# Transposing split queries and keys by float32r products with a unit matrix, in a kernel of two blocks on one core

## The chip, the core and the metric

The kernel runs on one core of a Trainium2 chip. Its metric is device time in microseconds, the median of several runs. Five engines work side by side, each through its own instructions in order: TensorE (PE; its loads of the stationary operand are listed as PEld), VectorE (DVE), ScalarE (ACT), GpSimd (POOL) and SyncE (SP), which here issues the loads from memory. TensorE writes to PSUM only, and other engines carry its results from there.

## What is computed

The reference runs two blocks of two layers each on 256 tokens of 1024 channels, with 256 tokens of context beside them. The change lies in the second block, in the mixers of its two layers. Both are attention over 64-wide heads whose queries and keys are normed by head and, for the latent tokens, rotated. The first layer ("even") has grouped heads, half of them with a window; the second ("odd") takes the difference of two attentions per head.

```python
def _odd_mixer(hx, hc, w_in, w_out, qn, kn, lq1, lk1, lq2, lk2, subln_w, lam_init, cos, sin, with_ctx):
    ...
    def heads(p, use_rope):
        b, n = p.shape[:2]
        q, k, v = jnp.split(p, [qs, 2 * qs], axis=-1)
        q = _rms(q.reshape(b, n, HEADS_C, 2, d), qn)
        k = _rms(k.reshape(b, n, HEADS_C, 2, d), kn)
        if use_rope:
            q, k = _rope(q, cos, sin), _rope(k, cos, sin)
        return q, k, v.reshape(b, n, HEADS_C, 2 * d)

    q_x, k_x, v_x = heads(hx @ w_in, True)
    q_c, k_c, v_c = heads(hc @ w_in, False)
    ...
    o_x = _diff_attend(q_x, jnp.concatenate([k_c, k_x], axis=1), jnp.concatenate([v_c, v_x], axis=1), lam)
```

All of it is float32. The kernel carries the large products in float32r, a float32 with fewer mantissa bits, and so splits each operand in two parts, hi (the rounded value) and lo (what is left), and adds three products.

## The kernel before

Activations lie with channels on partitions for the projections: aH and aL are hi and lo of the normed input. Weights come in by SyncE as 512 KB tiles wraw; ScalarE rounds them to whi (L392) and VectorE subtracts to get wlo (L397). mm3 (L411 to L413) issues the three products of hi and lo.

The attention needs queries and keys with the head's 64 channels on partitions, but their projection (tile pin, made by chunk) gives tokens on partitions. So qk (L1069) takes a chunk's result for two tiles of 128 tokens and four heads: a norm by head on VectorE, gains and rotation, the last product with the norm's factor at L1090, and then the split. For queries ScalarE rounds into q_st (L1093), and VectorE subtracts into its other half (L1094). For keys there is one tile k_st for each tile of tokens; ScalarE writes the hi part twice (L1106) and VectorE the lo part twice (L1107). Both tiles are float32r already, and share one pair of buffers.

The transposes come later (the function late that qk returns): stream runs them in the midst of the next chunk, after its third step. For each tile of tokens of queries there is one call of turned, and for keys two, one for hi (into ks0) and one for lo (into ks1). turned (L1123) issues four transposes of 128x128, one per head, into one PSUM bank (ptq), and ScalarE copies the bank into qs or ks (L1128):

```python
        pt = self.turn_tile(pp, "ptq")
        for h, a in enumerate(srcs):
            nc.tensor.transpose(out=pt[:, h, :], in_=a.bitcast(F32).rearrange("p e d -> p (e d)"), identity=self.ident)
        nc.scalar.copy(out=dst, in_=pt)
```

turn_tile (L1116) gives two banks by turns; the same two banks serve the transposes of the probabilities (ptp) and of the results (pto). scores (L1130) multiplies a query tile with ks0 and ks1 (L1134, L1135).

In the even layer the first k chunk, the v chunk and so on go pair of tiles by pair of tiles, and the later q chunks are woven into the attention of the group before. In the odd layer there are four pairs of heads j; while j's attention runs, the k and q chunks of j + 1 are woven in. So a pair has two sets of key transposes, 16 each (context, then latent tokens), and one of 8 for the queries.

The order on each engine is not the program's own order. A scheduler runs through the instructions by priority with durations that it assumes, and takes for each engine what is ready by then. The order is then fixed: on the chip each engine goes through it and waits wherever something is not ready.

Of the kernel before, what the change touches and what calls it, by code (L numbers as in the profile page):

```python
# [10 lines left out]
F32 = mybir.dt.float32  # L11
# [7 lines left out]
D = 1024  # L19
# [11 lines left out]
# columns of the per-partition vectors of a layer of the first block  # L31
# [7 lines left out]
# rows that are the same for each token, first block  # L39
RV = {"bv": (0, 512), "bs": (512, 256), "slg": (768, 256), "slb": (1024, 256)}  # L40
NRV = 1280
# the same, second block
# [3 lines left out]
# constants  # L46
CS = {"ident": (0, 128), "mf": (128, 128), "mb": (256, 128)}
NCS = 384
# constants of the first block's gates: selectors of a head's row, resets of the running sums
CG = {"sel": (0, 512), "reset": (512, 512)}  # L50
NCG = 1024
# norm gains
# [3 lines left out]
# form A tiles (128 columns) and form B chunks (256 columns) of the first block's input projection, in order  # L56
IN1 = ["gates", "k0", "k1", "k2", "k3", "q0", "q1", "q2", "q3", "V0", "V1", "a0", "g0", "a1", "g1", "u0", "u1", "S0",
       "o0", "o1", "o2", "o3"]
# how far an item of the first block's mixer falls behind in the order of priority
LOW, LOWC = 300, 600  # L60
# parts of the first layer's modulation that the tensor engine computes; the pairs of its shift tiles that it does as well
PE_C = [0, 1, 4]
SHPE = (1,)
# priority of the split of weights, by phase
WPRI = {"m1": 50, "ev": 400}
# other work per step of a phase, and the products woven into the attention's stages
PACE = {"m1": 0.0, "w1": 5.5, "o": 0.0, "f00": 5.0, "d00": 3.0, "f01": 1.0, "d01": 1.0, "f10": 3.0, "d10": 3.0}
RATE = {"ev": 0.7, "evo": 1.5, "od": 1.8, "odo": 1.0, "odv": 5.0}
# order of the work in the first block's mixer, by layer
# [18 lines left out]
class Net:  # L88
# [36 lines left out]
    # ---- modulation vectors: n on partitions, one dot product along the free axis each  # L125
# [6 lines left out]
    def cvec_pe(self, s, row):  # L132
        """The same for the first block, spread by the tensor engine."""
        nc = self.nc
        t = self.cv[s] = self.mp.tile([128, D], F32, tag="cv", name=f"cv0{s}")
        for h in range(2):
            p = self.mm_tile("pcv")
            nc.tensor.matmul(out=p, lhsT=self.ones[0:1, :], rhs=row[0:1, 512 * h:512 * h + 512], start=True, stop=True)
            nc.scalar.activation(out=t[:, 512 * h:512 * h + 512], in_=p, func=AF.Silu)
# [10 lines left out]
    def mod_gain(self, b, l, c, s):  # L150
        """A norm's gain times one plus the scale."""
# [4 lines left out]
    def mod_tile(self, b, l, j, streams, w=None):  # L156
        """Tile j of the 48 of a layer."""
# [14 lines left out]
    def mod_pe(self, c, q, room, pr, pm):  # L172
        """Tiles 2 q and 2 q + 1 of the first layer's part c on the tensor engine, for both streams: rows, then turned."""
# [12 lines left out]
    def mod_take(self, c, j0, j1, pm):  # L186
        """Tiles j0 to j1 of the part c, with the bias and with the norm's gain."""
# [10 lines left out]
    def start(self):  # L198
        """The first norm, tile by tile as its scales (on the tensor engine) and shifts become known."""
# [63 lines left out]
    def work(self, n):  # L263
        """Some of the modulation vectors that later layers need: as many dot products as credit allows."""
# [10 lines left out]
    def need(self, key):  # L275
        """The vectors of the key, and all before them in the queue."""
        while any(x[2] == key for x in self.bg):
            self.credit = self.bg[0][0]
            self.work(0.0)
# [4 lines left out]
    # ---- norms  # L284
    def rsq(self, x, n, scale, alone=False, x2=None, lim=None):
        """1 / sqrt(x * scale + eps) for [128, n]: a first guess from the exponent's bits, then two steps.
        With x2, then also 1 / sqrt(x2 + eps * (x * scale + eps)). With lim, 1 / sqrt(min(x, lim) + eps / scale)."""
# [18 lines left out]
        # the last step to the third order: y * (3/8 h^2 - 5/4 h + 15/8) with h = a * y^2  # L306
# [7 lines left out]
    def rstd_rows(self, sqs, n, scale, pc, pb, sqs2=None):  # L314
        """1 / sqrt(scale * (sum over partitions and tiles of sqs) + eps) for n tokens, on all partitions of pb.
        With sqs2, a second norm of the first one's result as well: the product of both factors, from the sums of the
        first one's squares and of those times its gains (and 1 / D)."""
# [15 lines left out]
    def squares(self, src, cols, scales=(None,)):  # L333
        """For each of the scales (by channel) two tiles whose sum over partitions is that of the squares over all channels."""
# [19 lines left out]
    def norm(self, src, cols, A, B, room=None):  # L354
        """aH + aL = src * rstd * A + B."""
# [25 lines left out]
    # ---- weights: loaded, split in two parts that one pass of the tensor engine carries exactly  # L381
# [18 lines left out]
    def more_weights(self, pool, n):  # L400
        """Further room for n weight tiles, from a pool of the phase."""
# [6 lines left out]
    def mm3(self, out, wh, wl, xh, xl, start, stop):  # L408
        """W.T @ x: weights stationary."""
# [5 lines left out]
    def accA(self, outs, ws, xs, cols, first=True, last=True):  # L415
        """For each output its weights; the pieces of the weights are [128, 128] each, for the tiles in xs."""
# [8 lines left out]
    def accB(self, out, ws, t):  # L425
        """x.T @ W: 128 tokens stationary; two pieces of weights, [128, 4, 256] each."""
# [11 lines left out]
    def order(n, colsets, head, tail):  # L438
        """Chunks by ranges of tokens; the first `head` and the last `tail` go range by range."""
# [7 lines left out]
    # ---- residual update by a projection: x += g * (W.T y)  # L447
# [11 lines left out]
    def part(self, p, w, ks, cols, first, last):  # L459
        """The tiles ks of a product over aH + aL, for the range of tokens cols."""  # L460
# [6 lines left out]
    def out_early(self, src, cols, ks):  # L467
        """The first tiles of a projection, as far as the tiles ks of its input reach."""
# [14 lines left out]
    def unscaled(self, pool, key):  # L483
        """The norm's input times its gains, without the factor by token, in two parts; the shifts as one more token.
        The first products take this, so that they need not wait for the factors."""
# [22 lines left out]
    def scaled(self, pool, p, rb, name):  # L508
        """A product with the unscaled input: times the factors by token, and the shifts' part."""
# [79 lines left out]
    # ---- the first block's mixer  # L589
    def mixer1(self, l, pace):  # L590
        nc, tc = self.nc, self.tc
        last = l == 1
        with ExitStack() as ctx:
# [43 lines left out]
            # rows 0..3: forward heads, 32..35: backward heads; the second half of the partitions likewise  # L637
# [10 lines left out]
            def interior(j):  # L648
                """Where the convolution's input goes: (context, latents) without the padding."""
# [61 lines left out]
            # -- the gates' running sums and maxima  # L711
            with tc.tile_pool(name="gp", bufs=1) as gp:
# [41 lines left out]
                # minus these, so that the selectors' minus makes it up  # L754
# [13 lines left out]
            # -- mLSTM chunks  # L768
# [10 lines left out]
            def step(c, d_, first, update, output):  # L779
# [4 lines left out]
                # minus M of each head, on all partitions  # L784
# [62 lines left out]
            def hnorm(c):  # L847
                """The sum of both directions, rms norm by head."""
# [8 lines left out]
            def gated(c):  # L857
                """The normed sum, times the output gate (into the gate's tiles)."""
# [106 lines left out]
    # ---- the second block  # L965
    def rows2(self, mx):
        rows = mx.tile([128, NR2], F32, name="rows")
        self.nc.sync.dma_start(out=rows, in_=self.i["rv2"].to_broadcast([128, NR2]))
        self.rot = mx.tile([128, 256], F32, name="rot")
# [3 lines left out]
    def tables(self, mx, rows, names, tag, scale=1.0):  # L973
        """Rotation tables with gains, [128, 2, 4, 64], for the head gains `names` (one, or one for each of four heads)
        times a power of two."""
# [19 lines left out]
    # ---- streams of instructions that are woven into each other; each yields what it has cost on the tensor engine  # L995
    def ahead(self, srcs):
        """Weights in order, each asked for one before its use."""
# [7 lines left out]
    def chunk(self, ws, toks, done):  # L1005
        """256 columns of an input projection for pairs of tiles of tokens; done gets each pair's result."""
# [15 lines left out]
    def fill_late(self, n):  # L1022
        """What waits for the vector engine's part of a chunk."""
# [5 lines left out]
    def stream(self, *parts):  # L1029
        """Chunks one after the other; what a chunk leaves to the tensor engine comes in the midst of the next one."""  # L1030
# [10 lines left out]
    def weave(self, main, fill, rate):  # L1041
        """rate: the fill's cost for one of main's."""
# [14 lines left out]
    def pipe(units):  # L1057
        """Software pipeline over units of four stages: (stage, cost) each."""
# [576 lines left out]
```

## Time and profile before

| | |
|---|---|
| median of 3 runs | 2061.7 us (2060.18 to 2063.29) |
| span of the profiled execution | 2055.1 us (the time around it is not listed apart) |
| instructions | 34137 |
| TensorE / VectorE / ScalarE busy | 2010.6 / 1545.2 / 924.5 us |
| mean granted TensorE clock | 0.994 |
| float32 transposes of L1127 | 256 records, from 1074.3 to 1818.1 us |

The span runs from the first to the last instruction of one profiled execution. Busy time of TensorE counts overlapping records once, and ends of its products are modelled, so its pace is read from the starts of successive rows. In a timeline, neighbouring instructions of one line are merged into a row with a count. An idle time stands in brackets behind a row, with what ended it.

### The profile page before, as it was taken

What the parts mean: (1) busy time and instruction counts of PE and PEld (TensorE: products, weight loads), DVE (VectorE), ACT (ScalarE), POOL (GpSimd) and SP (SyncE); (2) the same over time, 40 slices, a digit from 0 to 9 for tenths busy, and PEclk for the clock granted to TensorE, in tenths of its full rate; (3) what the DMA queues carried; (4) which work ended last, traced back from release to release, by engine and by line L of the source; (5) the groups of instructions that cost most, each with busy time, mean ns of one, the idle gap of its engine ahead of it and who ended that gap; (6) DMA issues with size and microseconds to landing.
All of it is one profiled execution on the core that took longest, in us unless ns stands there. A gap on an engine that the chain in (4) does not pass through costs nothing.

```text
span 2055.1 us, 34137 instructions
## 1 busy us (share of the span) xinstructions
PE 2010.6 (98%) x13196; PEld 1784.5 (87%) x13196; DVE 1545.2 (75%) x3105; ACT 924.5 (45%) x1612; POOL 85.7 (4%) x103
## 2 busy tenths in 40 slices
PE   8999999999999899999999999999999999999999
PEld 3798779888888799999998789888888889999999
DVE  6997789987898768987877667777653487788554
ACT  4324544222322346744556675322222266666443
POOL 0000010000001000200100002000000200001000
PEclk9999999999999999999999999999999999999999
DMA  7532265678766332576651015446752231216554
GB/s 295 181 103 92 97 232 176 211 248 295 235 216 198 111 102 94 170 263 212 202 171 61 22 41 186 154 149 223 260 170 71 70 112 64 73 54 224 182 157 134
DMA packets 98182, 324.22 MB, mean 158 GB/s; under 512 B 11418, under 2 KB 14234, under 8 KB 98020
## 3 DMA queue, kind: packets, MB, share of 16 engines
q1 hardware_dynamic: 98020, 322.04, 47.7%
q8 instruction: 104, 1.70, 0.3%
q14 instruction: 58, 0.48, 0.1%
HBM read 320.95 MB, written 1.05 MB: 157 GB/s over the span
## 4 chain that ended last, share of the span: by engine, by line
PE 89%; DVE 6%; ACT 2%; DMA 1%; issue 1%; SPq 0%; POOL 0%; ACTq 0%; POOLq 0%; DVEq 0%
PE pg L411 6%; PE pd L411 6%; PE pd L413 6%; PE pd L412 6%; PE pu L413 6%; PE pg L412 6%; PE pu L412 6%; PE pg L413 6%; PE pu L411 6%; PE pin L411 5%; PE pin L413 5%; PE pin L412 5%; PE pov L1223 2%; PE ptq L1127 2%; DVE wlo L397 1%; PE po L411 1%
## 5 line engine op out<-in xcount | busy, mean ns | idle before, releaser
L392 ACT CAST whi<-wraw 128x1024 fp32r<-128x1024 f32 (+2 forms) x443 | 429.5, 973 | 797.0 <-PE pu L412 188.9
L397 DVE TENSOR_TENSOR wlo<-wraw,whi 128x1024 fp32r<-128x1024 f32 (+2 forms) x443 | 502.5, 1138 | 155.0 <-ACT whi L392 152.3
L165 DVE CUSTOM_DVE_ANT_0 junk<-mw,cv,modb 128x1024 bf16<-128x1024 f32 x272 | 349.6, 1285 | 51.3 <-DMA mw<-in_modw 45.2
L411 PE MATMUL pd<-hH,whi 128*128 128x256 f32 (+1 forms) x748 | 245.4, 328 | 0.0
L412 PE MATMUL pd<-hL,whi 128*128 128x256 f32 (+1 forms) x748 | 245.1, 328 | 0.0
L413 PE MATMUL pd<-hH,wlo 128*128 128x256 f32 (+1 forms) x748 | 244.8, 327 | 0.0
L411 PE MATMUL pg<-aH,whi 128*128 128x256 f32 (+1 forms) x704 | 233.8, 332 | 0.3 <-ACT aH L374 0.3
L413 PE MATMUL pu<-aH,wlo 128*128 128x256 f32 (+1 forms) x704 | 233.5, 332 | 0.3 <-DVE wlo L397 0.3
L412 PE MATMUL pg<-aL,whi 128*128 128x256 f32 (+1 forms) x704 | 233.6, 332 | 0.0
L412 PE MATMUL pu<-aL,whi 128*128 128x256 f32 (+1 forms) x704 | 233.2, 331 | 0.0
L411 PE MATMUL pu<-aH,whi 128*128 128x256 f32 (+1 forms) x704 | 233.2, 331 | 0.0
L413 PE MATMUL pg<-aH,wlo 128*128 128x256 f32 (+1 forms) x704 | 233.2, 331 | 0.0
L412 PEld LDWEIGHTS pd<-hL,whi 128*128 128x128 f32 x748 | 142.2, 190 | 12.2
L411 PEld LDWEIGHTS pd<-hH,whi 128*128 128x128 f32 x748 | 142.4, 190 | 12.0
L413 PEld LDWEIGHTS pd<-hH,wlo 128*128 128x128 f32 x748 | 142.2, 190 | 12.0
L411 PE MATMUL pin<-whi,aH 128*128 128x256 f32 x512 | 150.0, 293 | 1.4 <-ACT aH L374 1.1
L412 PE MATMUL pin<-wlo,aH 128*128 128x256 f32 x512 | 148.0, 289 | 0.0
L413 PE MATMUL pin<-whi,aL 128*128 128x256 f32 x512 | 147.2, 289 | 0.3 <-DVE aL L375 0.2
L411 PEld LDWEIGHTS pg<-aH,whi 128*128 128x128 f32 x704 | 133.7, 190 | 13.2 <-ACT aH L374 0.5
L413 PEld LDWEIGHTS pu<-aH,wlo 128*128 128x128 f32 x704 | 133.7, 190 | 13.1 <-DVE wlo L397 0.5
L413 PEld LDWEIGHTS pg<-aH,wlo 128*128 128x128 f32 x704 | 133.8, 190 | 12.6
L412 PEld LDWEIGHTS pg<-aL,whi 128*128 128x128 f32 x704 | 133.8, 190 | 12.5
(339 smaller groups left out, 4150.8 us busy)
## 6 DMA issues: line engine op xcount, KB each, us to landing
wraw<-in_wgu SPq DMA_DIRECT2D x176, 512.0 KB, 4.4
mw<-in_modw SPq DMA_DIRECT2D x168, 512.0 KB, 4.2
wraw<-in_win SPq DMA_DIRECT2D x92, 512.0 KB, 3.5
wraw<-in_wdn SPq DMA_DIRECT2D x64, 384.0 KB, 3.5
wraw<-in_wout SPq DMA_DIRECT2D x47, 512.0 KB, 3.5
wraw<-in_wdn SPq DMA_DIRECT2D x64, 320.0 KB, 3.4
mn<-in_modn SPq DMA_DIRECT2D x18, 512.0 KB, 5.6
mn<-in_modw SPq DMA_DIRECT2D x6, 512.0 KB, 7.3
```

Source lines behind the costliest of these rows:

```text
L165: r = nc.vector.tensor_tensor_reduce(out=junk, in0=w, in1=self.cv[s], scale=1.0, scalar=self.mb_t[:, 2 * b + l, j:j + 1], op0=ALU.mult, op ...
L392: nc.scalar.copy(out=hi[:, :n], in_=raw[:, :n])
L397: nc.vector.tensor_tensor(out=lo[:, :n], in0=raw[:, :n], in1=hi[:, :n], op=ALU.subtract)
L411: mm(out=out, lhsT=wh, rhs=xh, start=start, stop=False)
L412: mm(out=out, lhsT=wh, rhs=xl, start=False, stop=False)
L413: mm(out=out, lhsT=wl, rhs=xh, start=False, stop=stop)
L1127: nc.tensor.transpose(out=pt[:, h, :], in_=a.bitcast(F32).rearrange("p e d -> p (e d)"), identity=self.ident)
L1223: nc.tensor.matmul(out=po[64 * b:64 * b + 64, e // 2, :], lhsT=vN[:, kc, 64 * g:64 * g + 64], rhs=u["PT"][:, kc, :], start=kc == 0, stop=k ...
```

## The change

A unit matrix in float32r is copied from the float32 one when a layer's attention begins, and turned issues ordinary products of the float32r tile with it in place of float32 transposes. The tile is the stationary operand both times and the matrix the moving one. The values are those of before, as every element is multiplied by one and added to zeros.

```diff
     def rows2(self, mx):
         rows = mx.tile([128, NR2], F32, name="rows")
         self.nc.sync.dma_start(out=rows, in_=self.i["rv2"].to_broadcast([128, NR2]))
+        self.unit = mx.tile([128, 128], F32R, name="unit")
+        self.nc.vector.tensor_copy(out=self.unit, in_=self.ident)
         self.rot = mx.tile([128, 256], F32, name="rot")
...
         pt = self.turn_tile(pp, "ptq")
         for h, a in enumerate(srcs):
-            nc.tensor.transpose(out=pt[:, h, :], in_=a.bitcast(F32).rearrange("p e d -> p (e d)"), identity=self.ident)
+            nc.tensor.matmul(out=pt[:, h, :], lhsT=a.rearrange("p e d -> p (e d)"), rhs=self.unit, start=True, stop=True)
         nc.scalar.copy(out=dst, in_=pt)
```

The other lines that the diff touches are comments. The scheduler's order shifts around the transposes; line numbers grow by two or three. On SyncE and GpSimd no row moves.

TensorE, the first set of keys of the even layer and the queries behind it, as a difference (L1127 is the transpose before, L1130 the product now; L411 to L413 are products of the projection that runs on beside them; unit and cst hold the unit matrix):

```order
-L1127 MATMUL ptq<-cst,k_st 128x128 x4
+L1130 MATMUL ptq<-unit,k_st 128x128 x4
 L413 MATMUL pin<-whi,aL_102 128x256
 L411 MATMUL pin<-whi,aH_95 128x256
 L412 MATMUL pin<-wlo,aH_95 128x256
+L1130 MATMUL ptq<-unit,k_st 128x128 x12
 L413 MATMUL pin<-whi,aL_103 128x256
 L411 MATMUL pin<-whi,aH_96 128x256
 L412 MATMUL pin<-wlo,aH_96 128x256
+L1130 MATMUL ptq<-unit,q_st 128x128 x8
 L413 MATMUL pin<-whi,aL_104 128x256
-L1127 MATMUL ptq<-cst,k_st 128x128 x4
```

The remaining three groups of keys moved up behind three products, and the queries behind three more; before, the next three groups of keys stand seven, two and four products apart.

TensorE, the second set of keys of the odd layer's head pair 2, before:

```order
L1127 MATMUL ptq<-cst,k_st 128x128 x4
L412 MATMUL pin<-wlo,aH_90 128x256
L413 MATMUL pin<-whi,aL_98 128x256
L411 MATMUL pin<-whi,aH_91 128x256
L412 MATMUL pin<-wlo,aH_91 128x256
L1127 MATMUL ptq<-cst,k_st 128x128 x8
L413 MATMUL pin<-whi,aL_99 128x256
L411 MATMUL pin<-whi,aH_92 128x256
L1127 MATMUL ptq<-cst,k_st 128x128 x4
```

Behind these stand ten products, the eight transposes of the queries, three products and then the first scores (L1134). The same place now, with the scores (L1137, L1138) behind it:

```order
L411 MATMUL pin<-whi,aH_89 128x256
L412 MATMUL pin<-wlo,aH_89 128x256
L1130 MATMUL ptq<-unit,k_st 128x128 x16
L413 MATMUL pin<-whi,aL_97 128x256
L1130 MATMUL ptq<-unit,q_st 128x128 x8
L1137 MATMUL S<-ks_17778,qs 128x512
L1138 MATMUL S<-ks_17779,qs 128x512
```

All sixteen of the keys stand in a row, one product parts them from the eight of the queries, and the scores follow these at once. In the first set of the same pair, groups of 4, 8 and 4 with six and two products between them became 4 and 12 with three between them.

## Rows read from the trace of the kernel before

**Rows 1.** The page, its parts 1 and 4: busy time and the chain by engine.

```profile
PE 2010.6 (98%) x13196; PEld 1784.5 (87%) x13196; DVE 1545.2 (75%) x3105; ACT 924.5 (45%) x1612; POOL 85.7 (4%) x103
...
PE 89%; DVE 6%; ACT 2%; DMA 1%; issue 1%; SPq 0%; POOL 0%; ACTq 0%; POOLq 0%; DVEq 0%
```

**Rows 2.** Stretches of time: length, busy time by engine, PEclk, DMA share, GB/s.

```profile
1075.00:1100.00 25.00, 24.98 (x202) 23.10 (x201) 21.34 (x56) 18.54 (x38) 0.00 (x0) 1.00 0.27 90
...
1760.00:1800.00 40.00, 39.77 (x312) 37.59 (x311) 30.25 (x87) 26.56 (x54) 0.00 (x0) 1.00 0.21 68
```

**Rows 3.** Line 1127, keys: count, duration in ns (min/median/max), first and last start.

```profile
L1127 PEld LDWEIGHTS ptq<-cst,k_st x160: 137/141/145, 1074.3 to 1815.7; 128*128 128x128 f32 x160
L1127 PE MATMUL ptq<-cst,k_st x160: 270/273/330, 1074.3 to 1815.8; 128*128 128x128 f32 x160
```

**Rows 4.** Timeline of TensorE, even layer: start, length in us, engine, line.

```profile
1076.27 0.28 PE L412 MATMUL pin<-wlo,aH 128*128 128x256 f32 x1
1076.39 0.60 PE L1127 MATMUL ptq<-cst,k_st 128*128 128x128 f32 x4
1076.74 0.36 PE L413 MATMUL pin<-whi,aL 128*128 128x256 f32 x1
1076.94 0.28 PE L411 MATMUL pin<-whi,aH 128*128 128x256 f32 x1
```

**Rows 5.** Timeline of TensorE at 600 us, products of 512 columns.

```profile
600.02 0.39 PE L412 MATMUL pu<-aL,whi 128*128 128x512 f32 x1
600.24 0.39 PE L413 MATMUL pu<-aH,wlo 128*128 128x512 f32 x1
600.47 0.39 PE L411 MATMUL pu<-aH,whi 128*128 128x512 f32 x1
```

**Rows 6.** Timeline of TensorE, plain float32 products and the next instruction.

```profile
1692.88 1.10 PE L1371 MATMUL pov<-vN,PT 128*128 128x128 f32 x8
1693.74 0.36 PE L411 MATMUL pin<-whi,aH 128*128 128x256 f32 x1
```

**Rows 7.** Timeline of TensorE's loads: eight of 128 columns for one-column products.

```profile
807.04 0.97 PEld L323 LDWEIGHTS pcv<-ones,csq 128*128 128x128 f32 x8
```

**Rows 8.** Loads of float32r products, by form: count, busy us, mean ns, idle.

```profile
L412 PEld LDWEIGHTS pin<-wlo,aH 128*128 128x128 f32 x512 | 98.3, 192 | 2.3 <-issue 1.4
```

**Rows 9.** Timeline of TensorE, odd layer, pair 2: the changed line alone.

```profile
1762.53 0.66 PE L1127 MATMUL ptq<-cst,k_st 128*128 128x128 f32 x4
...
1763.73 1.03 PE L1127 MATMUL ptq<-cst,k_st 128*128 128x128 f32 x8
...
1765.01 0.66 PE L1127 MATMUL ptq<-cst,k_st 128*128 128x128 f32 x4
...
1768.62 0.60 PE L1127 MATMUL ptq<-cst,k_st 128*128 128x128 f32 x4
...
1769.54 1.04 PE L1127 MATMUL ptq<-cst,k_st 128*128 128x128 f32 x8
...
1770.81 0.66 PE L1127 MATMUL ptq<-cst,k_st 128*128 128x128 f32 x4
...
1772.63 1.06 PE L1127 MATMUL ptq<-cst,q_st 128*128 128x128 f32 x8
```

**Rows 10.** Timeline of VectorE, the same pair: lo parts of keys and queries.

```profile
1762.80 1.28 DVE L1107 TENSOR_TENSOR k_st<-q_t,k_st 128x512 fp32r<-128x512 f32 x2
...
1768.52 1.28 DVE L1107 TENSOR_TENSOR k_st<-q_t,k_st 128x512 fp32r<-128x512 f32 x2
1771.80 0.69 DVE L1094 TENSOR_TENSOR q_st<-q_t,q_st 128x512 fp32r<-128x512 f32 x1 [1.99 <-ACT q_st L1093]
```

**Rows 11.** Timeline of ScalarE, the same pair: copies out of PSUM, the queries' cast.

```profile
1769.26 0.58 ACT L1128 CAST ks<-ptq 128x512 fp32r<-128x512 f32 x1 [0.43 <-PE ptq L1127]
1770.17 1.07 ACT L1128 CAST ks<-ptq 128x512 fp32r<-128x512 f32 x2 [0.33 <-PE ptq L1127]
1771.13 0.63 ACT L1093 CAST q_st<-q_t 128x512 fp32r<-128x512 f32 x1
```

## Prediction

> **What bounds the kernel now.** I read the page first, then the clock by stretches, then the changed line, then the rates of its neighbours, and last the three engines around one set of transposes. TensorE is busy 98% of the span and makes up 89% of the chain that ended last [rows 1]. In the two stretches of the attention stages that hold changed instructions it is busy 24.98 of 25 us and 39.77 of 40 us, at a granted clock of 1.00, the upper of its two levels [rows 2]. So whatever one of its instructions costs there, or however long it stands, goes into the time. The pace between starts matters here, not the recorded durations, because matmul records overlap.
>
> **Part 1: the instruction itself.** The change touches 256 instructions: 160 on k_st [rows 3] and, by the loops, 96 on q_st. Four of them cost this much: the float32r product ahead starts at 1076.27, the four at 1076.39, the next products at 1076.74 and 1076.94. From 1076.27 to 1076.94 are 0.67 us, of which two ordinary products of 0.12 each would have taken 0.24 [rows 4]. The other 0.43 to 0.44 us go to four transposes: 0.109 us each. A float32 transpose is one record here, not two, so it is already cheap.
>
> No row has a float32r product of 128 columns, so I bound it. *From below:* the stream. Products of 512 columns start 0.225 us apart (600.02, 600.24, 600.47) [rows 5] and products of 256 columns 0.12 apart [rows 4]. So 256 columns more cost 0.106, and 128 columns would take 0.12 - 0.053 = 0.067. *From above:* the plain float32 product of the same size. Four of them (each two records, hence x8) take from 1692.88 to 1693.74, 0.215 each [rows 6]. *Between:* the load of the stationary part, which here changes with every product. A run of eight loads of 128 columns, each followed by a product with a single column, takes 0.97 us; without the last one's own 0.19 that is 0.78 / 7 = 0.111 per load [rows 7]. With one column there is nothing to stream, so this pace is the load's. The float32r loads have the same recorded length, 192 ns [rows 8] against the 0.19 us of these, where the transposes' load takes 141 [rows 3].
>
> I take 0.112 us, since the new load is nearest to rows 7 and 8. That is 3 ns more than now, times 256 = **+0.8 us**. Ends kept for the range: 0.067 (-42 ns x 256 = -10.8 us) and 0.215 (+106 ns x 256 = +27.1 us). A rule speaks for the lower end. The Trainium skill (TensorE: Matmul & The Clock Gate, section on weight-path perf modes) has a fast load switched on for 128 weights of any type but FP32; if float32r counts as another type, the stream would set the pace and this term would be -10.8. The equal load lengths of rows 8 speak against it, and no run here has shown a short float32r load.
>
> **Part 2: what moves.** The order of instructions shifts around the transposes, and this I hold to be the larger cost. Before, groups of four are separated by products, which cover the ScalarE copy that empties a PSUM bank; there are two banks by turns. Now up to sixteen stand in a row, then one product, then eight more, as shown above. I work one head pair through, from the trace of TensorE [rows 9], VectorE [rows 10] and ScalarE [rows 11]. Constants: four transposes 0.44; their last result 0.60 after the first start when not held up; a copy 0.59, beginning 0.04 later; TensorE resumes some 0.05 after it.
>
> *First set of the pair (k, now 4, three products, 12).* The first group starts at 1762.53, so TensorE is free at 1763.33. The second group needs the first of the two k_st differences, done at 1762.80 + 0.64 = 1763.44: it starts at 1763.50. The third may follow at 1763.94, as the first bank's copy is over by 1763.82. The fourth waits for the second bank: results at 1764.10, copy over at 1764.70, start at 1764.74 instead of 1764.38. Waits 0.17 + 0.36 = 0.53. Before, the fourth started at 1765.01 after 0.44 + 6 x 0.12 + 0.87 + 2 x 0.12 = 2.27 from 1762.53, a wait of 0.2. Added: 0.33.
>
> *Second set (k 16 in a row, one product, q 8).* First group 1768.62; second when the difference is done, 1769.20 instead of 1769.06; third after the first copy, 1769.90 instead of 1769.64; fourth after the second copy, 1770.48 instead of 1770.34. ScalarE then has the q_st cast (0.63 [rows 11]) ahead of the two last k copies, and VectorE's q_st difference (0.69 [rows 10]) follows that cast, so the first q group starts at about 1771.85 instead of 1771.04. Waits 0.14 + 0.26 + 0.14 + 0.81 = 1.35. Before: 0.16 ahead of 1770.81 and 0.18 ahead of 1772.63, together 0.34. Added: 1.01. Behind the q groups the score products now follow at once, where three products stood: they need the first q copy, over at about 1773.1, while TensorE is free at 1772.73; that is some 0.4, against 0.1 before. Added: 0.3.
>
> Sum for a pair: 0.33 + 1.01 + 0.3 = 1.65; head pairs 1, 2 and 3 of the odd layer have the same rows: 3 x 1.65 = 4.95. Three other places bunch alike (both k sets of the even layer, the first with its q; the second k set of the odd layer's pair 0): I put each at the pair's two sets, 0.33 + 1.01 = 1.34, an estimate: 4.02. The even layer's other q groups keep products between them or stand eight in a row as before: 0. **Together +9.0 us.** Between 3 (VectorE and ScalarE reach their parts earlier than in the trace of before, since their rows shift too) and 14 (the places that I did not work cost twice as much).
>
> **Part 3: the rest.** The unit matrix takes one VectorE copy of 128x128 per attention layer, below the 0.64 of a 128x512 difference [rows 10]; TensorE has products to do there: 0, at worst 0.5. SyncE's and GpSimd's rows are the same in both orders, so no transfer moves.
>
> **Sum.** +0.8 + 9.0 = +9.8. Against the profiled execution: 2055.1 to 2064.9 us of span. That span lies 6.6 below the median 2061.7 of the three runs; with the same 6.6 around it: **2071.5 us**, +0.48%.
>
> **Rivals.** *Forecast (0.57):* load pace and bunching, 2066 to 2078 us.
>
> *A, the stream sets the pace (0.12), the case that can end faster.* Mechanism: the load of the next stationary part hides wholly behind products, at 0.067 us each. Price -10.8. The waits of part 2 remain, as they hang on copies and differences: -10.8 + 9.0 gives 2059.9; if half of them go, 2055.4. The point from which it decides: with 9.0 of waits a product must be below 0.109 - 9.0 / 256 = 0.074 us to be faster than now. Against it: rows 7 and 8. For it: products of 256 columns, whose loads are recorded no longer than 192 ns either, show no extra time for them at 0.12.
>
> *B, the banks keep up (0.18).* Same pace as forecast, but VectorE and ScalarE are early enough that only 1 to 3 us of the waits are real: 2063.5 to 2065.5, no measurable change. For it: ScalarE has idle time of 0.3 to 0.4 us around these copies [rows 11]. Against it: two banks and 0.59 a copy cannot feed a group per 0.44.
>
> *C, the product is carried as a float32 one, in two records (0.13).* Then 0.215 each, +27.1; a group then takes 0.86, longer than a copy, and the bunching costs little: 2088.8. For it: the wider float32r products are the only ones in the trace, so none shows a narrow one in one record. The Trainium skill (Perfetto Trace Analysis, section Transposes) also wants logical transposes done as transposes, because these skip the arithmetic; by it the change loses, but it gives no figure. That the change does nothing (same instruction under another name) would leave the pace at 0.109 and is covered by the forecast's waits.
>
> **How the numbers follow.** A measurement of this kernel can tell about 0.2%, 4.1 us: faster means below 2057.6, slower above 2065.8. Faster: most of A with half the waits, 0.08. No difference: the rest of A, B, and the forecast's low edge, 0.22. Slower: the remaining forecast and C, 0.70. The range 2058 to 2080 takes in the forecast's own 2066 to 2078, B and part of A, and leaves out C and A's low end.
>
> **What would show it.** Right: 256 records at the changed line, loads near 190 ns instead of 141; sixteen in a row taking clearly more than 16 x 0.112 = 1.8 us; TensorE idle ahead of them that ends on ks copies or VectorE's k_st. Wrong: groups of four in 0.27 us (A), or 512 records (C), or no new idle time at the changed line (B).

## The result and the profile after

The changed kernel takes 2080.56 us (median of 4 runs, 2077.62 to 2083.26); the kernel before, run beside it, 2060.94. The ratio is 1.0096, 95% interval 1.0080 to 1.0112: **slower by 19.6 us** where I had forecast 9.8, and just above the end of my range.

The page of the changed kernel, parts 1 and 4, busy time and chain by engine:

```profile
PE 2023.3 (97%) x13196; PEld 1797.1 (87%) x13196; DVE 1545.4 (74%) x3107; ACT 926.9 (45%) x1612; POOL 83.9 (4%) x103
...
PE 85%; DVE 9%; ACT 2%; issue 2%; DMA 1%; SPq 0%; POOL 0%; POOLq 0%; ACTq 0%; DVEq 0%
```

TensorE's share of the chain fell from 89 to 85%, VectorE's rose from 6 to 9% [rows 1]. The same two stretches as in [rows 2]:

```profile
1075.00:1100.00 25.00, 24.17 (x173) 23.29 (x172) 18.56 (x55) 14.97 (x24) 0.00 (x0) 0.86 0.40 127
...
1760.00:1800.00 40.00, 37.71 (x272) 35.48 (x271) 28.77 (x84) 24.77 (x46) 0.00 (x0) 0.91 0.20 67
```

TensorE is idle in them, and its granted clock, the column behind the busy times, is no longer 1.00 throughout: a part of each stretch ran at the lower of its two levels (1.2 and 2.4 GHz). The view of the changed line (1127 before, 1130 now), its records and what ended the idle time ahead of them:

```profile
L1130 PEld LDWEIGHTS ptq<-unit,k_st x160: 186/192/333, 1078.2 to 1833.9; 128*128 128x128 f32 x160
L1130 PE MATMUL ptq<-unit,k_st x160: 223/275/415, 1078.2 to 1834.0; 128*128 128x128 f32 x160
...
  ACT ks L1131: 8.4, 20
  ACT k_st L1108: 6.2, 9
  DVE q_st L1096: 2.6, 4
  DVE k_st L1109: 2.3, 6
```

(These are the largest of nine entries.) There is one record for each product, loads take 192 ns where [rows 3] have 141, and 24 us of idle time in all stand ahead of the line where there were 2.8. The load's longest, 333 ns, is one at the lower clock level.

The span grew by 22.2 us (2077.3 against 2055.1), but 3.9 of these lie ahead of the first changed instruction (1078.2 against 1074.3), where both kernels run the first block. Executions differ there; so I measure each profile from its first transpose on. The marks are the changed line's first row in the even layer, the norm product of L331 that begins the way to the odd layer, the changed line's first rows in the odd layer's pairs 0 to 3, the last scores and the end: 1074.3, 1638.3, 1666.7, 1718.1, 1762.5, 1807.0, 1830.1, 2055.1 before, and 1078.2, 1646.2, 1672.1, 1726.9, 1775.5, 1825.5, 1853.6, 2077.3 after. Pair 1 for instance: (1775.5 - 1726.9) - (1762.5 - 1718.1) = 4.1 (4.14 with another digit). Longer than before, in us:

| kernel | even layer | way to odd | pair 0 | pair 1 | pair 2 | pair 3 | behind | sum |
|---|---|---|---|---|---|---|---|---|
| changed | 4.0 | -2.5 | 3.4 | 4.1 | 5.5 | 5.1 | -1.4 | 18.3 |
| changed, again (e11) | 3.1 | -2.5 | 3.5 | 5.7 | 4.4 | 6.6 | -0.9 | 19.8 |
| e1 products, old order | 0.0 | 0.1 | 0.1 | 0.1 | 0.1 | 0.1 | -0.4 | 0.1 |
| e2 float32 transposes, new order | 6.1 | -2.7 | 3.5 | 3.1 | 3.1 | 4.0 | -1.3 | 15.9 |
| e3 products, old order on TensorE alone | 1.3 | -1.3 | 0.6 | -0.1 | -0.2 | 0.6 | -0.4 | 0.6 |
| e4 float32r transposes, own order | -3.7 | 0.1 | -1.1 | -0.6 | -0.6 | -0.2 | -0.4 | -6.4 |
| e5 float32r transposes, old order | -1.3 | -2.4 | -0.2 | -0.4 | -0.4 | -0.2 | 0.2 | -4.7 |
| e6 late, bunched | 3.9 | -2.6 | 3.5 | 3.1 | 3.1 | 4.9 | 0.1 | 16.1 |
| e12 the same again | 3.1 | -2.6 | 3.5 | 4.6 | 2.1 | 5.9 | -0.5 | 16.2 |
| e7 float32r transposes, new order | 2.2 | 0.2 | 3.4 | 4.1 | 3.8 | 6.1 | -1.3 | 18.4 |
| e8 early, spaced | 4.0 | -2.5 | 3.5 | 2.1 | 2.1 | 3.8 | 0.9 | 13.8 |
| e9 pairs 1 to 3 put back | 3.1 | 0.2 | 3.6 | -0.1 | -0.1 | 0.6 | -0.3 | 7.0 |
| e10 all but these put back | 1.3 | -0.1 | 0.6 | 5.5 | 4.3 | 6.5 | -1.3 | 16.9 |

The way to the odd layer holds none of the 256 instructions, only the unit copy on VectorE, and yet some profiles are 2.4 to 2.7 us shorter there than that of before. The granted clock of this stretch (0.88 and 1.00) goes with it; before, after, and e5:

```profile
1638.00:1667.00 29.00, 26.47 (x171) 24.29 (x172) 24.68 (x79) 13.93 (x26) 0.73 (x1) 0.88 0.25 92
...
1646.00:1672.00 26.00, 23.45 (x168) 21.15 (x169) 24.08 (x79) 13.39 (x26) 0.73 (x1) 1.00 0.33 103
...
1636.00:1662.00 26.00, 23.25 (x166) 20.94 (x167) 24.05 (x80) 13.23 (x26) 0.74 (x1) 1.00 0.33 103
```

That the fall there hangs on the change is not shown, so costs of the even layer are read below without this column; the sums contain it. Of e2's 6.1 in the even layer, about 3 lie at 1270 to 1280 us, without any of the 256 instructions and at a mean granted clock of 0.83.

### The profile page after: what moved, and what is told of

The parts are those of the page before. It is cut to its first block, busy times and chain, and to the rows that moved or that the text cites. A ratio compares the mean times of both kernels' runs of the same rounds, so it can differ in the third digit from the quotient of the medians.

```text
span 2077.3 us, 34141 instructions
## 1 busy us (share of the span) xinstructions
PE 2023.3 (97%) x13196; PEld 1797.1 (87%) x13196; DVE 1545.4 (74%) x3107; ACT 926.9 (45%) x1612; POOL 83.9 (4%) x103
## 4 chain that ended last, share of the span: by engine, by line
PE 85%; DVE 9%; ACT 2%; issue 2%; DMA 1%; SPq 0%; POOL 0%; POOLq 0%; ACTq 0%; DVEq 0%
PE pg L411 6%; PE pu L413 6%; PE pu L412 6%; PE pg L412 6%; PE pu L411 6%; PE pg L413 6%; PE pd L412 6%; PE pd L411 6%; PE pd L413 6%; PE pin L411 4%; PE pin L413 4%; PE pin L412 4%; DVE wlo L397 2%; PE pov L1226 2%; PE ptp L1145 1%
## 5 line engine op out<-in xcount | busy, mean ns | idle before, releaser
L411 PE MATMUL pd<-hH,whi 128*128 128x256 f32 (+1 forms) x748 | 244.6, 327 | 0.0
L413 PE MATMUL pd<-hH,wlo 128*128 128x256 f32 (+1 forms) x748 | 244.0, 326 | 0.0
L413 PE MATMUL pu<-aH,wlo 128*128 128x256 f32 (+1 forms) x704 | 233.4, 332 | 0.3 <-DVE wlo L397 0.3
L411 PE MATMUL pg<-aH,whi 128*128 128x256 f32 (+1 forms) x704 | 233.6, 332 | 0.0
L411 PE MATMUL pu<-aH,whi 128*128 128x256 f32 (+1 forms) x704 | 233.1, 331 | 0.0
L413 PE MATMUL pg<-aH,wlo 128*128 128x256 f32 (+1 forms) x704 | 233.1, 331 | 0.0
L411 PEld LDWEIGHTS pd<-hH,whi 128*128 128x128 f32 x748 | 141.6, 189 | 12.2
L413 PEld LDWEIGHTS pd<-hH,wlo 128*128 128x128 f32 x748 | 141.5, 189 | 12.0
L411 PE MATMUL pin<-whi,aH 128*128 128x256 f32 x512 | 150.2, 294 | 1.4 <-ACT aH L374 1.1
L413 PE MATMUL pin<-whi,aL 128*128 128x256 f32 x512 | 147.3, 289 | 0.5 <-DVE aL L375 0.4
L413 PEld LDWEIGHTS pu<-aH,wlo 128*128 128x128 f32 x704 | 133.7, 190 | 12.9 <-DVE wlo L397 0.5
L411 PEld LDWEIGHTS pg<-aH,whi 128*128 128x128 f32 x704 | 133.7, 190 | 12.9 <-ACT aH L374 0.2
L411 PEld LDWEIGHTS pu<-aH,whi 128*128 128x128 f32 x704 | 133.8, 190 | 12.6
L412 PEld LDWEIGHTS pu<-aL,whi 128*128 128x128 f32 x704 | 133.8, 190 | 12.4
```

What stands on the lines that cost most here:

```text
L411: mm(out=out, lhsT=wh, rhs=xh, start=start, stop=False)
L412: mm(out=out, lhsT=wh, rhs=xl, start=False, stop=False)
L413: mm(out=out, lhsT=wl, rhs=xh, start=False, stop=stop)
```

## Experiments

**Theory 1**: the instruction costs about the same, and the order that the scheduler gives around it costs the rest. **Theory 2**: the instruction itself does, by its longer load or by what it does to the clock. To part them, an order is imposed: edges that only fix which instruction an engine issues next, without a wait.

```diff
+def pin(tc, nc, free):
...
+        for a, b in zip(order, order[1:]):
+            tc.add_manual_dep(b, a.name, info, reason="pin")
```

**e1, the new instruction in the old order.** The edit is the lines above, with the order of before for three engines.

> The changed kernel (float32r products with the unit matrix), but with TensorE, VectorE and ScalarE in the second block issuing in exactly the order of the kernel before, by added ordering edges; the same instructions as the changed kernel. Theory 1 (the order costs it, the instruction hardly anything): the time of the kernel before plus 0.8 us, ratio 1.000 to 1.002; idle time of TensorE ahead of the changed line back to about 3 us from 24. Theory 2 (the instruction costs it, by its longer load or by a granted clock that falls beside it): within 4 us of the changed kernel, ratio 1.008 or more. In between (1.003 to 1.007): both.

Measured: 2059.74 us against 2059.55, ratio 0.9997 (0.9987 to 1.0007). Of the view of the changed line:

```profile
L1130 PEld LDWEIGHTS ptq<-unit,k_st x160: 186/192/192, 1075.8 to 1817.7; 128*128 128x128 f32 x160
...
  issue: 0.9, 5
  ACT k_st L1108: 0.3, 1
  ACT qs L1131: 0.2, 1
```

The loads are as long as after the change, yet the idle time is gone. Theory 2 falls for this order: the 256 products cost 0.1 us together in the profile, and the interval of the whole runs takes in 1.

**e2, the old instruction in the new order.** The same lines on the kernel before.

> The kernel before (float32 transposes), but with TensorE, VectorE and ScalarE in the second block issuing in exactly the order of the changed kernel. Theory 1 (the order): about 2080, ratio 1.008 to 1.011, with TensorE idle ahead of the transposes for some 20 us instead of 2.8. Theory 2 (the instruction): as the kernel before, ratio 0.998 to 1.002.

Measured: 2077.61, ratio 1.0077 (1.0061 to 1.0094). The view of the line:

```profile
L1127 PEld LDWEIGHTS ptq<-cst,k_st x160: 137/141/144, 1082.5 to 1836.7; 128*128 128x128 f32 x160
...
  ACT ks L1128: 11.0, 23
  ACT k_st L1106: 8.1, 11
  DVE k_st L1107: 3.2, 10
  DVE q_st L1094: 2.8, 4
```

The same waits with an unchanged instruction: the order makes them. But the pairs 1 to 3 take 3.1 to 4.0 us more, and 4.1 to 6.6 in the changed kernel. The rest goes with the clock. Pair 2 of the changed kernel, from 4.5 us behind its first transpose on:

```profile
1780.00:1790.00 10.00, 8.18 (x41) 7.16 (x41) 4.78 (x9) 6.20 (x12) 0.00 (x0) 0.73 0.00 0
```

and the same place of e2, whose pair 2 begins at 1780.7:

```profile
1785.00:1795.00 10.00, 7.81 (x53) 6.34 (x52) 5.33 (x12) 6.32 (x13) 0.00 (x0) 1.00 0.00 0
```

TensorE is idle for no less in e2 (2.2 us against 1.8). Over whole runs e2 has a mean granted clock of 0.991 to 0.995 (six runs), the changed kernel 0.988 to 0.991 (nine).

**e3, TensorE alone put back.** The order table of e1 for TensorE only.

> The changed kernel with TensorE alone put back to the order of the kernel before in the second block; VectorE and ScalarE keep what order the scheduler then gives them (120 and 52 places differ from before). If the loss comes from where TensorE's transposes stand (theory 1): ratio 1.000 to 1.003. If the earlier or later places of the casts, differences and bank copies on VectorE and ScalarE make it: 1.004 or more, and the idle time ahead of the changed line stays above 10 us. If the instruction makes it (theory 2): 1.008 or more.

Measured: 2063.83, ratio 1.0018 (1.0004 to 1.0031), 0.6 us in the second block of its profile (1.9 without the way to the odd layer). The order on TensorE makes most of it. The places in which VectorE and ScalarE still differ from before cost 0.8 to 6.4 us by the interval of the whole runs; the profile is of one of the shorter runs (2059.29).

**e4, float32r transposes in the scheduler's own order.**

```diff
-            nc.tensor.matmul(out=pt[:, h, :], lhsT=a.rearrange("p e d -> p (e d)"), rhs=self.unit, start=True, stop=True)
+            nc.tensor.transpose(out=pt[:, h, :].bitcast(F32R), in_=a.rearrange("p e d -> p (e d)"), identity=self.unit)
```

> The kernel before with its 256 transposes kept as transposes but fed as float32r with the float32r unit matrix, in the scheduler's own order, which then hardly differs from before's. If the pace of a transpose is set by its load (0.111 us for 128 columns): the time of before, ratio 0.999 to 1.002, records of the load near 190 ns. If one pass of 128 columns at float32r's rate sets it (0.067 us): 42 ns x 256 = 10.8 us less, ratio 0.995. If it is handled as a float32 one: no change at all, load 141 ns.

Measured: **2053.91 us, ratio 0.9967 (0.9956 to 0.9978)**, faster than both. The loads in the view of its line:

```profile
L1130 PEld LDWEIGHTS ptq<-unit,k_st x160: 137/140/146, 1077.7 to 1813.1; 128*128 128x128 f32 x160
```

A group of four in the timeline of TensorE, with the products around it:

```profile
1812.84 0.28 PE L411 MATMUL pin<-whi,aH 128*128 128x256 f32 x1
1812.96 0.47 PE L1130 MATMUL ptq<-unit,k_st 128*128 128x128 f32 x4
1813.26 0.35 PE L412 MATMUL pin<-wlo,aH 128*128 128x256 f32 x1
1813.45 0.28 PE L413 MATMUL pin<-whi,aL 128*128 128x256 f32 x1
```

Worked as [rows 4] were: from 1812.84 to 1813.45 are 0.61, less 0.24 for two products 0.37, that is 92 ns a transpose where there were 109. The load is as long as that of a float32 transpose, 140 ns, yet the pace is quicker: none of the three outcomes that I had written down.

**e5, float32r transposes in the old order.**

> Float32r transposes as in e4_rt_own, with all three engines in exactly the order of the kernel before. Third of a series in one order: float32 transposes (before), float32r products (e1_new_old_order), float32r transposes (this). In e4_rt_own they started about 85 ns apart in undisturbed rows, against 109. Theory 1 (the pace counts where no wait covers it): 24 ns x 256 = 6 us less than before, ratio 0.996 to 0.998. Rival (the gain of e4_rt_own came from its slightly other order): ratio 0.999 to 1.001.

Measured: 2055.27, ratio 0.9984 (0.9975 to 0.9994), 4.7 us less in the second block of its profile. Of these 4.7, 2.4 lie on the way to the odd layer, where the clock did not fall. So in one and the same order float32 transposes, float32r products and float32r transposes take 0, 0.0 and -2.3: 2.3 over 256 is 9 ns each, about half of the 17 between 109 and 92. The 6 us of theory 1 counted the undisturbed pace for all 256; that the profile came near is in part luck, and the ratio of the whole runs stayed just above its 0.998. e4's profile has the clock of before on that way (0.1 in the table), so its gain of 6.4 is not the clock's there. By e5 more than half of it is not the instruction's either: e4's order differs from that of before (104 instructions stand ahead of the scores of pairs 1 and 2, where before has 93), and suits the even layer (-3.7 against -1.3) and pair 0 (-1.1 against -0.2) better. What in that order does it wasn't followed up.

**e6 and e8, a part of the cover put back.** Both keep the changed kernel's TensorE order except in the odd layer's pairs 1 to 3. In e6 the second set moves nine products back, still bunched:

```
 L411 MATMUL pin<-whi,aH_89 128x256
 L412 MATMUL pin<-wlo,aH_89 128x256
-L1130 MATMUL ptq<-unit,k_st 128x128 x16
...
 L411 MATMUL pin<-whi,aH_92 128x256
 L412 MATMUL pin<-wlo,aH_92 128x256
+L1130 MATMUL ptq<-unit,k_st 128x128 x16
```

> The changed kernel in its own order, but in the odd layer's head pairs 1, 2 and 3 the second set's row of sixteen, the queries and the scores move 9 products back, so that 26 products again lie between the two sets; the sixteen still stand in a row. Theory 1, made exact (every product that the order took from between the first set and the scores was cover, 0.12 us each, because the data behind casts and copies come no earlier): 3 x 9 x 0.12 = 3.2 us less than the changed kernel, ratio to before 1.007 to 1.009 where the changed kernel has 1.0096; the wait of 1.03 us ahead of each second set is gone, the other waits stay. Rival (the two banks set it, as I worked it in the prediction): nothing gained, ratio 1.009 to 1.011, the wait only moves to the groups behind.

Measured: 2083.34, ratio 1.0115 (1.0100 to 1.0130). In the view of the line the casts' share went and nothing took its place:

```profile
  ACT ks L1131: 8.4, 20
  DVE q_st L1096: 2.6, 4
  DVE k_st L1109: 2.1, 6
...
  ACT k_st L1108: 1.1, 3
```

The cast's 6.2 fell to 1.1, and the three pairs take 11.1 instead of 14.8 us longer. The clean figure is pair 1, in which both have a mean granted clock of 0.96: 3.06 against 4.14, that is 1.08, or 9 x 0.12. In e8 the set stays early, but is spaced by 18 products:

```
-L1130 MATMUL ptq<-unit,k_st 128x128 x16
+L1130 MATMUL ptq<-unit,k_st 128x128 x4
...
+L1130 MATMUL ptq<-unit,k_st 128x128 x8
...
+L1130 MATMUL ptq<-unit,k_st 128x128 x4
```

> The changed kernel in its own order, but in head pairs 1, 2 and 3 of the odd layer 18 products go back to between the groups of the second set, its queries and the scores (groups of 4, 8, 4 and 8 with 4, 2, 10 and 3 products between); the set itself stays early, 17 products behind the first. Theory 1, made exact (0.12 us of cover for each product): 3 x 18 x 0.12 = 6.5 us less than the changed kernel, ratio to before 1.005 to 1.008; the wait of about 1.03 us ahead of each second set stays, those behind it go. Rival (bunching costs what I forecast, 1.35 + 0.3 for a pair's second set and scores): 3 x 1.3 to 1.65 = 4 to 5 us less, ratio 1.007 to 1.008. Second rival (the loss lies elsewhere, in the even layer or the clock): no change, 1.009 to 1.011.

Measured: 2076.38, ratio 1.0090 (1.0074 to 1.0106); the three pairs 8.0 us longer, 6.7 less than changed. That this is near theory 1's 6.5 is luck: in e8's pairs the granted clock stayed at 1.00, and against e2, which has the changed kernel's order at that clock (10.3), the spacing gains only 2.3, not 0.12 for each product. These waits are left:

```profile
  ACT k_st L1108: 6.2, 9
  ACT ks L1131: 4.6, 11
```

In the profiles e6 moved the pairs as theory 1 said, and e8 by its waits a third as far; in whole runs neither gained clearly: the intervals overlap with that of the changed kernel. So I ran e6 again.

**e12, e6 once more.**

> The kernel of e6_late_bunched once more, because its two readings disagree: in its profile the three head pairs took 3.6 us less than in the changed kernel's, as theory 1 said, while its run times (ratio 1.0115) were no better. Theory 1: pairs 1 to 3 together 10 to 13 us longer than before (changed kernel 14.8 and 16.6), scores beginning 10.8 us behind a pair's first transpose as before, and, if the run times of e6_late_bunched were chance from the stretch ahead of the second block, a ratio of 1.006 to 1.009. If the ratio is again 1.010 or more, then moving nine products gains nothing in whole runs, whatever one profile shows.

Measured: 2077.11, ratio 1.0092 (1.0078 to 1.0106): the 1.0115 of e6 did not come again, but neither is a gain of 3 us over the changed kernel (1.0096, 1.0093) shown by run times. The profile gives a reason. Three of its stretches, inside pairs 1, 2 and 3 in turn:

```profile
1730.00:1740.00 10.00, 8.98 (x50) 8.18 (x49) 4.22 (x9) 6.54 (x13) 0.00 (x0) 0.73 0.01 2
1780.00:1790.00 10.00, 8.75 (x61) 7.68 (x60) 4.99 (x10) 7.38 (x15) 0.00 (x0) 1.00 0.00 0
...
1830.00:1840.00 10.00, 9.98 (x50) 9.34 (x51) 5.08 (x12) 6.52 (x18) 0.00 (x0) 0.66 0.00 0
```

Pair 2, in which the clock stayed up, is 2.1 us longer than before; pair 1, with the same rows, 4.6. The fall of the clock costs 2.5 in this pair (a mean of 0.93 over it; in pair 1 of the changed kernel, with 0.96, 1.0 against e2), and whether it comes differs from pair to pair and from one execution to the next.

**e7, float32r transposes in the new order.**

> Float32r transposes, as in e5_rt_old_order, with all three engines in exactly the order of the changed kernel. Theory 1 (the order sets the time; a faster transpose only waits longer): ratio 1.006 to 1.010, as e2_old_new_order with its 1.0077, since the waits take up what the pace gives. Theory 2 (the instruction sets it): ratio below 1.002. Also open: whether the granted clock falls in 1780 to 1790 us as it did with float32r products (0.73) and not with float32 transposes (1.00) in the same order. If float32r is what matters it falls here too, if product against transpose is, it does not.

Measured: 2078.07, ratio 1.0092 (1.0078 to 1.0107). The faster instruction of e4 and e5 saves nothing in whole runs here: the waits take it up. And the clock falls. The same place of pair 2 as above (it begins at 1778.4 here):

```profile
1783.00:1793.00 10.00, 7.44 (x46) 6.15 (x45) 4.75 (x10) 6.46 (x13) 0.00 (x0) 0.83 0.00 0
```

Over its six runs the mean granted clock is 0.986 to 0.990.

**e9, e10 and e11, where it lies.** The old order on TensorE in pairs 1 to 3 alone, everywhere but there, and the changed kernel again.

> The changed kernel with TensorE put back to the order of the kernel before in the odd layer's head pairs 1 to 3 alone; the even layer and pair 0 keep the changed order. The second block (from its first transpose to the end of the span) was 18.3 us longer than before in the profile of the changed kernel, 16.1 in e6_late_bunched (27 products put back), 13.8 in e8_early_spaced (54 back), 0.6 in e3_new_old_pe (all back). Theory 1, made exact (cover taken away, at most 0.12 us for each of 3 x 32 products): 18.3 - 11.5 = 7 us longer than before, ratio 1.002 to 1.005. Rival (the loss is the even layer's and pair 0's, or the granted clock's): above 12 us, ratio over 1.006.

> The complement of e9_pairs_back: TensorE in the order of before in the even layer and pair 0, in the changed order in pairs 1 to 3. Theory 1: the second block 11 to 12 us longer than before, ratio 1.004 to 1.007, and with e9_pairs_back's excess it adds up to the changed kernel's 18.3 within 3 us. Rival: under 6 us, ratio below 1.003.

> The changed kernel unaltered, on the same chip as e9_pairs_back and e10_rest_back: it gives the time they are compared with, and a second profile of the second block. Theory 1 and its rival both expect a ratio of 1.008 to 1.011. If the 18.3 us of its second block hold, the figures read from one profile each can be set side by side; if it differs by over 3 us, differences below that are noise.

Measured: 1.0030 (1.0018 to 1.0042), 1.0098 (1.0081 to 1.0115) and 1.0093 (1.0077 to 1.0110). e9's 7.0 came as expected, but in part by luck: putting the pairs back took away 14.4 us and not 11.5, as the clock no longer fell in them (1.00), and 2.6 came back on the way to the odd layer. The pairs 1 to 3 hold most of the loss. e10 came out higher than expected, 16.9 instead of 11 to 12: I had priced the pairs by their waits and again not by the clock, and in its pairs the clock fell. e9 and e10 add up to 23.9, 4 to 6 above the whole; 2.6 of that is the way to the odd layer, where both have the clock of before.

## Why the prediction was right and wrong

**Part 1 was right.** Where nothing holds them up, products in one row start 0.109 to 0.115 us apart, around the 0.112 taken, and e1 prices all 256 at 0.1 us, not 0.8. Rivals A and C fall with it. By the Trainium skill's rule of a fast load of 128 weights for any type but FP32 (TensorE: Matmul & The Clock Gate, weight-path perf modes) the time would have been rival A's, if float32r counted as another type; the trace doesn't show that fast load for float32r products, whose loads are recorded with 192 ns as in [rows 8].

**Part 2 was right in kind and wrong in size.** The new idle time ends on copies, casts and differences, as named. The failed step is the second set's *"first group 1768.62"*: I left it at its old time. But the new order puts it 17 products behind the first set instead of 26, so TensorE comes there 9 x 0.12 = 1.08 us early, and what it needs is no earlier. The timeline of TensorE in the changed kernel, pair 2:

```profile
1775.48 0.66 PE L1130 MATMUL ptq<-unit,k_st 128*128 128x128 f32 x4
...
1780.29 0.28 PE L412 MATMUL pin<-wlo,aH 128*128 128x256 f32 x1
1781.32 0.66 PE L1130 MATMUL ptq<-unit,k_st 128*128 128x128 f32 x4 [0.75 <-ACT k_st L1108]
1782.31 1.08 PE L1130 MATMUL ptq<-unit,k_st 128*128 128x128 f32 x8 [0.33 <-DVE k_st L1109]
1783.62 0.67 PE L1130 MATMUL ptq<-unit,k_st 128*128 128x128 f32 x4 [0.23 <-ACT ks L1131]
1784.12 0.33 PE L413 MATMUL pin<-whi,aL 128*128 128x256 f32 x1
1784.96 1.94 PE L1130 MATMUL ptq<-unit,q_st 128*128 128x128 f32 x8 [0.51 <-DVE q_st L1096]
1786.72 0.79 PE L1137 MATMUL S<-ks,qs 128*128 128x512 f32 x1
```

ScalarE in the same place, the cast that the first of these waits for:

```profile
1780.65 1.14 ACT L1108 CAST k_st<-q_t 128x512 fp32r<-128x512 f32 x2 [1.53 <-DVE nw_u L310]
```

and its row in the kernel before:

```profile
1767.69 1.15 ACT L1106 CAST k_st<-q_t 128x512 fp32r<-128x512 f32 x2 [1.40 <-DVE nw_u L310]
```

Counted from the pair's first transposes (1775.48 now, 1762.53 in [rows 9]) the cast begins 5.17 us in, and 5.16 before. TensorE's order changed; the chain on ScalarE and VectorE did not get shorter. Start to start, less the normal distance, the waits of this pair compare so with mine: first set 0.49 (0.53 forecast); first group of the second set 1.03 - 0.12 = 0.91 (0); second group 0.61 - 0.11 = 0.49 (0.14); the groups behind 0.39 (0.40); queries 0.84 - 0.12 = 0.72 (0.81). So most terms were near, one was missing, and one was short. For a pair I had added 1.65; at the full clock e2 measures 3.1 (pairs 1 and 2).

A shorter account would have caught it. In the kernel before, pair 2's first scores come here:

```profile
1773.94 0.50 PE L1134 MATMUL S<-ks,qs 128*128 128x512 f32 x1
```

That is 11.41 us behind its first transposes, with 93 instructions of TensorE before them (transposes included). With 61 in e2 it is 10.76 (1780.67 to 1791.44), with 70 in e12 10.78, with 79 in e8 11.13. Hardly anything moves the scores, since they wait for the chain. So 32 products taken from ahead of them are 32 x 0.12 = 3.84 us of work that must be done later, for 0.65 gained: 3.2 us lost per pair, and e2 shows 3.1 in each of pairs 1 and 2. With 9 put back it is 23 x 0.12 - 0.63 = 2.1, and e12 shows 2.1 in the pair with the full clock. In e8 it would be 14 x 0.12 - 0.28 = 1.4 and 2.1 were measured; the waits behind its scores that may explain the rest weren't followed up.

The same count prices pair 0, which I had put at 1.34 without working it. Its first scores before and after:

```profile
1684.38 0.50 PE L1134 MATMUL S<-ks,qs 128*128 128x512 f32 x1
...
1689.97 0.49 PE L1137 MATMUL S<-ks,qs 128*128 128x512 f32 x1 [0.23 <-ACT qs L1131]
```

That is 17.65 us behind its first transposes with 145 instructions ahead of them, and 17.86 with 116. So 29 products moved and nothing was gained: 29 x 0.12 + 0.21 = 3.7, and 3.4 to 3.6 were measured.

**What I had not priced at all is the clock.** I counted every term at the upper level. In the changed kernel's pairs TensorE's idle stretches are followed by products at the lower one: the eight of the queries take from 1784.96 to 1786.72, 0.22 us each instead of 0.112. Pair by pair the changed kernel stands 1.0 to 2.5 us above e2, which has the same order at the full clock. For pairs 1 to 3 the sum is 14.8, of which by this comparison e2's 10.3 are waits and 4.5 clock.

The places that I did not work: pair 0 cost 3.4 to 3.5 instead of 1.34, the even layer 3.1 to 4.0 instead of 2 x 1.34 (its own fall of the clock included). My upper bound doubled these and not the pairs that I had worked, so 14 was too low. Part 3 held: TensorE waits 0.5 us for the unit copy at one norm product (L323), and in the kernel before it waits 0.5 for another VectorE row at the same line. Rival B's early engines did not appear.

## What to carry to other kernels

Where a scheduler moves consumers on the bounding engine, count the work that stands ahead of each wait before and after, and compare its sum with how much sooner the chain on the other engines can end; work taken from in front of a fixed chain comes back as idle time at full price. Part an instruction's cost from its order by running the new instruction in the old order and the old one in the new: here the first was free and the second cost nearly all. And try the neighbouring form of the operation: transposes kept as transposes, in float32r, beat both kernels.

## What the runs showed of the hardware that I had not expected

Float32r transposes of 128 columns cost 92 ns each in the group above, float32 transposes 109 [rows 4], float32r products with the same unit matrix about as much as these; over all 256, waits included, the gain in one order was 9 ns each. Their loads are recorded with 140, 141 and 192 ns, so the length of the load alone doesn't tell the pace. The Trainium skill (Perfetto Trace Analysis, section Transposes) asks for logical transposes to be done as transposes; for float32r the trace agrees, with 2.3 us between e1 and e5 in one order (ratios 0.9997 and 0.9984 in whole runs), while float32 transposes and float32r products cost the same (0.1 us over 256). No run here shows why.

After idle time the granted clock fell with float32r products (0.73 in the ten microseconds of pair 2 shown above) and with float32r transposes (0.83), and stayed at 1.00 with float32 transposes in the same order and with as much idle time; no load of e2's line is longer than 144 ns. It didn't fall in the pairs of e8 either, where TensorE was idle for less, nor in pair 2 of e12, whose instructions are float32r products too. These are single profiles, so that the kind of instruction decides is not shown; what sets the fall off stays open.
